# Conformer and forgetting-attention trunk: the shared filter sum moved to ScalarE and GpSimd ahead of the chunk, the memory matrices in split passes

## The chip, the core and the metric

The kernel runs on one core of a Trainium2 chip. Its time is the device time of one execution in microseconds. The engines are TensorE (PE; PEld for its weight loads), VectorE (DVE), ScalarE (ACT), GpSimd (POOL) and the DMA queue of SyncE (SP).

## What is computed

```python
for l in range(2):                                  # layer 0: convolution, layer 1: attention
    if l == 0:                                      # Conformer convolution
        u = h @ w_pw1 + b_pw1                       # 1024 tokens x 1024 -> 2 x 1024
        u = a * sigmoid(gate)
        u = causal depthwise convolution, 31 taps per channel, + b_dw
        x = x + silu(layernorm(u)) @ w_pw2 + b_pw2
    else:
        x = x + fox_attention(rmsnorm(x))           # 16 heads, shared keys and values
    mem_n = rmsnorm(mem)                            # 256 memory tokens
    k, v = mem_n @ w_k, mem_n @ w_v                 # 4 heads of 256
    x = x + softmax(q @ k.T) @ v @ w_o              # cross-attention, q = rmsnorm(x) @ w_q
    x = x + relu(rmsnorm(x) @ w1)**2 @ w2           # 4096 wide
return rmsnorm(x)
```

All is float32. A product may be taken in one pass over plain float32 operands, or each operand is split into a high part (type fp32r) and a low part (the rest), and three passes low x high, high x low, high x high are summed.

## The kernel before

Channels lie on the 128 partitions, tokens on the free axis; the 1024 channels make 8 chunks and the 1024 tokens two halves of 512. This text is about the first stage, `conv_layer`, in the first 527 us of the span; what follows it (memory attention, feed-forward, attention) is not touched.

For each chunk `gated_unit` makes the gated input u: four products of 24 matmuls (128x512, split operands), a sigmoid on ACT and a combining step on DVE for each half of the tokens. The tokens are stored as even and odd ones. `convolve` then filters the chunk: with d0 and d1, two differences of even and odd tokens, and `both`, a shared sum of 16 terms, every output half is `both` plus 16 (first half) or 15 (second half) terms from d0 or d1. Each term is one DVE instruction (`scalar_tensor_tensor`: source times a tap plus the running sum). After the last chunk `layer_norm` works on each half, and the product with `pw2` follows.

Beside it runs `memory_matrices`, a generator: for each of 2 layers and 4 heads it makes kt and vt (memory tokens times w_k, w_v), and from them with w_q and w_o the matrices mqk and mvo, which are stored to DRAM through a tile `o` with 2 buffers. It is advanced by one step (kt; vt; the w_q part; the w_o part) with each `next(prep)`: twice for each chunk, and what is left after `layer_norm`. The weights come through tiles `praw`.

The kernel is written in a tile language: instructions of one engine stay in the order that a scheduler fixes when the kernel is built, engines wait for one another by semaphores, and a tile's buffer is taken again when its last reader is done. Many short-lived tiles share one group of 4 buffers (`tag="t"`), taken in turn in the order of the program. PSUM has 8 banks; the preparation had 4 of them, the gate 2, small things 2.

Of the kernel before, what the change touches and what calls it, by code (L numbers as in the profile page):

```python
# [86 lines left out]
def trunk(ctx, tc, a, out):  # L87
# [98 lines left out]
    def add_squares(acc, ch):  # L186

        sq = nrm.tile([P, HALF], F32, name="sq", tag="t", bufs=4)
# [103 lines left out]

    def conv_layer(pm, prep):
        with tc.tile_pool(name="conv", bufs=2) as cp:
# [90 lines left out]

    def convolve(cp, m, u, sums):


        n, k = S // 2, TAPS // 2
        even, odd = u[:, 0, :], u[:, 1, :]  # L390
        d0 = cp.tile([P, n + k], F32, name="d0")
        d1 = cp.tile([P, n + k - 1], F32, name="d1")
        dve.tensor_tensor(d0, even[:, : n + k], odd[:, : n + k], op=ALU.subtract)
        dve.tensor_tensor(d1, even[:, 1 : n + k], odd[:, : n + k - 1], op=ALU.subtract)
        both = cp.tile([P, n], F32, name="both")
        dve.tensor_scalar(
            both, odd[:, :n], sums[:, 0:1], col("dw_b", m), op0=ALU.mult, op1=ALU.add
        )
        for j in range(1, k + 1):
            dve.scalar_tensor_tensor(  # L400
                both, odd[:, j : j + n], sums[:, j : j + 1], both, op0=ALU.mult, op1=ALU.add
            )
        out = [X[:, m, sl] for sl in HALVES]
        for s, d, taps in ((0, d0, k + 1), (1, d1, k)):
            y = both
            for j in range(taps):
                w = col("dw_w", m * TAPS + 2 * j + s)
                dve.scalar_tensor_tensor(  # L408
                    out[s], d[:, j : j + n], w, y, op0=ALU.mult, op1=ALU.add
                )  # L410
                y = out[s]

# [20 lines left out]
    def memory_matrices(pp, pq, layer):  # L433
# [3 lines left out]

        def get(src):
            raw = pp.tile([P, NCH, P], F32, name="praw", bufs=3)
            nc.sync.dma_start(raw, src)  # L440
            return raw

        mem = pp.tile([P, NCH, MEM], F32, name="mem", bufs=1)
        nc.sync.dma_start(mem, a["memT"])
        if layer == 0:
            r = inverse_rms([mem[:, c, :] for c in range(NCH)], RMS_EPS)
# [3 lines left out]
        for c in range(NCH):  # L450
            act.activation(mem[:, c, :], mem[:, c, :], AF.Copy, scale=col(f"src{layer}", c))
        for h in range(MEM_HEADS):
            kv = []
            for w, n in ((wk, "kt"), (wv, "vt")):
                t = bank(pq).rearrange("p (c m) -> p c m", c=2)
                for c in range(2):
                    x = get(w[2 * h + c])
                    product(t[:, c, :], [((x[:, k, :],), (mem[:, k, :],)) for k in range(NCH)])
                o = pp.tile([P, 2, MEM], F32, name=n, bufs=1)
                if w is wk:  # L460
# [8 lines left out]
                kv.append(o)  # L469
                yield  # L470
            kt, vt = kv
            for j in range(2):

                x = get(wq[h, j])
                for g in range(2):
                    t = bank(pq).rearrange("p (f m) -> p f m", f=2)
                    o = pp.tile([P, 4, P], F32, name="o").rearrange("p (f b) n -> p f (b n)", f=2)
                    for f in range(2):
                        product(t[:, f, :], [
                            ((x[:, 4 * c + 2 * g + f, :],), (kt[:, c, :],)) for c in range(2)  # L480
                        ])
# [6 lines left out]
            for j in range(2):  # L488

                x = get(wo[h, j])  # L490
                for mc in range(2):
                    t = bank(pq)
                    product(t, [
                        (
                            (vt[:, c, mc * P : (mc + 1) * P],),
                            (x[:, 4 * c : 4 * c + 4, :].rearrange("p b n -> p (b n)"),),
                        )
# [864 lines left out]

    with prep_pools(4) as pools, banks(2) as pm:
        conv_layer(pm, chain(*(memory_matrices(*pools, l) for l in range(2))))
    sums = mem_attention(0)
# [80 lines left out]
```

## Time and profile before

| | |
|---|---|
| median of 3 runs | 2822.05 us (2818.59 to 2823.66) |
| the profiled execution | 2825.31 us, span 2823.3 us |
| busy in the span | PE 2740.8 us, PEld 2261.3, DVE 2030.9, ACT 1278.3, POOL 703.1 |
| 80 to 388 us (filters of the 8 chunks) | PE 303.89 of 308, DVE 302.63, ACT 63.08, POOL 0.75 |
| 388 to 431 us (layer norm) | PE 41.68 of 43, DVE 31.63, ACT 27.98, POOL 2.01 |
| 431 to 527 us (pw2) | PE 96.00 of 96, DVE 41.30, ACT 33.10, POOL 0 |

Rows of groups give the line, engine, operation, output and inputs, the count after x, then the busy time in us, the mean duration of one in ns, and the idle time before them with what ended it. Matmuls are pipelined, so the mean of one is longer than the distance from one to the next. A plain float32 matmul shows as two records. Rows of a timeline give start in us, length in us, and the instructions that were merged. In rows of the order that the scheduler fixed, a name's number tells tiles of the same name apart.

### The profile page before, as it was taken

The numbers are of one execution on the slowest core, as the hardware profiler recorded it, in microseconds if no ns is written. First come the engines' busy times: TensorE is split into PE (matmuls) and PEld (weight loads), VectorE is DVE, ScalarE is ACT, GpSimd is POOL, SyncE is SP. The second block draws the span as 40 slices with busy tenths as digits, with TensorE's granted clock in tenths as the row PEclk, the third lists the DMA queues.
The fourth block names the chain that finished last, engine by engine and source line by source line (L and its number), as shares of the span: only waits on it lengthen the run. The fifth ranks groups of instructions, "written<-read, shape, count | busy, mean of one in ns | idle before, by whom it ended". The sixth has DMA issues, their size and how long they took to land.

```text
span 2823.3 us, 36214 instructions
## 1 busy us (share of the span) xinstructions
PE 2740.8 (97%) x12968; PEld 2261.3 (80%) x12968; DVE 2030.9 (72%) x3358; ACT 1278.3 (45%) x2293; POOL 703.1 (25%) x473
## 2 busy tenths in 40 slices
PE   8999999999999999999899999989999999989998
PEld 6777777888888877888688888878888788878886
DVE  5999984555776576777788888875546855577776
ACT  5212143433555553333466666673423655543332
POOL 0000000000065625774000000000000365525773
PEclk9999999999999999999899999999999999999999
DMA  6334364322165585652222221243213455655651
GB/s 219 120 119 135 114 206 124 101 90 70 65 230 177 178 309 187 227 199 89 69 68 70 57 65 55 69 136 98 94 64 105 149 176 190 218 208 197 227 201 61
DMA packets 165428, 390.68 MB, mean 138 GB/s; under 512 B 17264, under 2 KB 46192, under 8 KB 164992
## 3 DMA queue, kind: packets, MB, share of 16 engines
q1 hardware_dynamic: 165248, 388.37, 40.9%
q8 instruction: 102, 1.67, 0.2%
q14 instruction: 78, 0.64, 0.1%
HBM read 270.79 MB, written 113.31 MB: 136 GB/s over the span
## 4 chain that ended last, share of the span: by engine, by line
PE 74%; DVE 12%; ACT 5%; DMA 5%; issue 3%; POOL 1%; SPq 0%; DVEq 0%; POOLq 0%; ACTq 0%
PE mm L1070 34%; PE mm L269 29%; PE mm L1255 5%; DVE w L148 2%; DVE op L148 2%; DVE x L408 1%; PE mm L1341 1%; DVE x L1310 1%; DMA ua<-x 1%; ACT x L1315 1%; PE mm L1353 1%; PE mm L1354 1%; DVE both L400 1%; DVE wl L148 1%; ACT pth L151 1%
## 5 line engine op out<-in xcount | busy, mean ns | idle before, releaser
L1070 PE MATMUL mm<-op,w 128*128 128x512 f32 x5424 | 1242.4, 391 | 24.5 <-ACT m L955 8.7
L1070 PEld LDWEIGHTS mm<-op,w 128*128 128x128 f32 x5424 | 1020.5, 189 | 243.2 <-ACT m L955 9.6
L269 PE MATMUL mm<-op,wh 128*128 128x512 f32 x1056 | 330.5, 394 | 4.2 <-DVE op L148 4.2
L148 DVE TENSOR_TENSOR w<-r,w 128x512 fp32r<-128x512 f32 x264 | 262.6, 998 | 30.5 <-ACT w L653 30.5
L653 ACT CAST w<-r 128x512 fp32r<-128x512 f32 x264 | 163.3, 622 | 262.0 <-PE mm L1070 233.2
L269 PEld LDWEIGHTS mm<-op,wh 128*128 128x128 f32 x1056 | 200.2, 190 | 48.5 <-DVE op L148 6.5
L1255 PE MATMUL mm<-op,wh 128*128 128x512 f32 x736 | 231.4, 396 | 0.0
L148 DVE TENSOR_TENSOR w<-t,w 128x512 fp32r<-128x512 f32 x180 | 178.2, 1005 | 63.2 <-ACT w L653 63.1
L269 PE MATMUL mm<-op,wl 128*128 128x512 f32 x528 | 210.5, 400 | 7.1 <-DVE wl L148 6.2
L207 POOL TENSOR_TENSOR r<-v,mhalf 128x4 f32<-128x4 f32 (+1 forms) x15 | 16.8, 1117 | 741.0 <-DVE v L205 741.0
L647 POOL TENSOR_TENSOR t<-r,t 128x512 f32<-128x512 f32 x104 | 174.9, 1681 | 91.4 <-DVE w L148 54.2
L653 ACT CAST w<-t 128x512 fp32r<-128x512 f32 x180 | 112.0, 622 | 169.8 <-PE mm L1070 140.6
L151 ACT CAST wh<-raw 128x1024 fp32r<-128x1024 f32 x96 | 100.7, 1050 | 193.8 <-PE mm L269 97.5
L865 POOL TENSOR_TENSOR x<-x,x 128x512 f32<-128x512 f32 x112 | 160.2, 1455 | 112.6 <-ACT x L878 101.6
L967 DVE TENSOR_TENSOR x<-mm,x 128x512 f32<-128x512 f32 x160 | 109.5, 684 | 91.1 <-PE mm L1070 73.7
L1255 PEld LDWEIGHTS mm<-op,wh 128*128 128x128 f32 x736 | 139.2, 189 | 26.7
L269 PE MATMUL mm<-op,xsh 128*128 128x512 f32 x512 | 158.0, 393 | 0.0
L1255 PE MATMUL mm<-op,wl 128*128 128x512 f32 x368 | 155.0, 421 | 1.9 <-ACT q L1275 1.9
L151 ACT CAST pth<-mm 128x512 fp32r<-128x512 f32 (+1 forms) x224 | 105.9, 495 | 108.5 <-PE mm L556 80.8
L408 DVE SCALAR_TENSOR_TENSOR x<-d,par,x 128x512 f32<-128x512 f32 x232 | 154.5, 746 | 0.0
L647 POOL TENSOR_TENSOR t<-r,r 128x512 f32<-128x512 f32 x52 | 80.2, 1542 | 295.1 <-DMA r<-in_ff_w 191.0
L1315 ACT ACTIVATE x<-x,nb 128x128 f32<-128x128 f32 (+7 forms) x128 | 99.5, 778 | 109.3 <-DVE nb L1313 100.0
(188 smaller groups left out, 4689.6 us busy)
## 6 DMA issues: line engine op xcount, KB each, us to landing
r<-in_ff_w SPq DMA_DIRECT2D x128, 512.0 KB, 4.0
op<-ua SPq DMA_DIRECT2D x80, 512.0 KB, 6.8
us<-x SPq DMA_DIRECT2D x128, 256.0 KB, 2.9
op<-us SPq DMA_DIRECT2D x64, 512.0 KB, 5.6
raw<-mvo SPq DMA_DIRECT2D x32, 512.0 KB, 3.4
ua<-ul SPq DMA_DIRECT2D x64, 256.0 KB, 2.2
ua<-uh SPq DMA_DIRECT2D x60, 256.0 KB, 2.3
raw<-in_pw SPq DMA_DIRECT2D x24, 512.0 KB, 4.7
```

The costliest lines, as they stand in the source:

```text
L148: dve.tensor_tensor(lo, src, hi.bitcast(F32), op=ALU.subtract)
L151: act.copy(hi, src)
L269: pe.matmul(out_ps, x, y, start=i == 0, stop=i == len(terms) - 1)
L400: dve.scalar_tensor_tensor(both, odd[:, j : j + n], sums[:, j : j + 1], both, op0=ALU.mult, op1=ALU.add)
L408: dve.scalar_tensor_tensor(out[s], d[:, j : j + n], w, y, op0=ALU.mult, op1=ALU.add)
L647: (dve if g in (2, 3, UP, UP + 1) else pool).tensor_tensor(t, raws[g, x], raws[g, y], op=ALU.subtract)
L653: act.copy(highs[n][0], raws[steps[n][:2]])
L865: eng.tensor_tensor(u[g, x], y1, y2, op=op_)
L967: dve.tensor_tensor(v, sums[key], v, op=ALU.add)
L1070: pe.matmul(sums[key], y, z, start=first and i == 0, stop=n == last_of[key] and i == len(terms) - 1, skip_group_check=True,)
L1255: pe.matmul(t, x, y, start=n == 0, stop=n == len(terms) - 1)
L1315: act.activation(x[:, :n], x[:, :n], AF.Exp, bias=nb, accum_out=rs)
```

## The change

- The shared sum becomes a function of its own, `shared_sum`: ACT multiplies (16 instructions), and POOL adds (15), in place of 16 instructions on DVE. It is issued, with the gate of the next chunk, before the filters of the chunk at hand. The products of ACT go through the tiles of the group "t".
- The two filter chains of a chunk run one after the other with their running sum in one PSUM bank (pool `pc`), no longer in X; only the last step writes X. d0 and d1 have one buffer instead of two.
- The preparation takes its products in three split passes. Weights come as two half pieces, each cast on ACT (high part), the low part subtracted on DVE for the first half piece and on POOL for the second. kt and vt are split too (kt by way of a tile of the group "t"), and the memory tokens. Its PSUM banks go from 4 to 3.

```diff
@@ conv_layer
+            ready = u, shared_sum(cp, 0, u, pairs[:, 0])
             for m in range(NCH):
-                if m:
-                    u = padded()
-                    for sl in HALVES:
-                        gated_unit(pm, cp, m, ahead, hs, u[:, :, PAD // 2 :], sl)
+                now = ready
                 if m + 1 < NCH:
                     ahead = gate_weights(m + 1)
                 for _ in range(2):
                     next(prep, None)
-                convolve(cp, m, u, pairs[:, m])
+                if m + 1 < NCH:
+                    u = padded()
+                    for sl in HALVES:
+                        gated_unit(pm, cp, m + 1, ahead, hs, u[:, :, PAD // 2 :], sl)
+                    ready = u, shared_sum(cp, m + 1, u, pairs[:, m + 1])
+                convolve(cp, pc, m, *now)
...
+    def shared_sum(cp, m, u, sums):
+        n, k = S // 2, TAPS // 2
+        odd = u[:, 1, :]
+        both = cp.tile([P, n], F32, name="both")
+        act.activation(both, odd[:, :n], AF.Identity, scale=sums[:, 0:1], bias=col("dw_b", m))
+        for j in range(1, k + 1):
+            t = nrm.tile([P, HALF], F32, name="tap", tag="t", bufs=4)
+            act.activation(t, odd[:, j : j + n], AF.Copy, scale=sums[:, j : j + 1])
+            pool.tensor_tensor(both, both, t, op=ALU.add)
+        return both
@@ convolve
-        out = [X[:, m, sl] for sl in HALVES]
+        acc = bank(pc)
         for s, d, taps in ((0, d0, k + 1), (1, d1, k)):
             y = both
             for j in range(taps):
+                o = X[:, m, HALVES[s]] if j == taps - 1 else acc
                 w = col("dw_w", m * TAPS + 2 * j + s)
-                dve.scalar_tensor_tensor(
-                    out[s], d[:, j : j + n], w, y, op0=ALU.mult, op1=ALU.add
-                )
-                y = out[s]
+                dve.scalar_tensor_tensor(o, d[:, j : j + n], w, y, op0=ALU.mult, op1=ALU.add)
+                y = acc
@@ memory_matrices
         def get(src):
-            raw = pp.tile([P, NCH, P], F32, name="praw", bufs=3)
-            nc.sync.dma_start(raw, src)
-            return raw
+            halves = []
+            for i in range(2):
+                raw = half(src[:, 4 * i : 4 * i + 4, :])
+                hi, lo = (pp.tile([P, NCH // 2, P], F32R, name=f"p{x}", bufs=3) for x in "hl")
+                act.copy(hi, raw)
+                (pool if i else dve).tensor_tensor(lo, raw, hi.bitcast(F32), op=ALU.subtract)
+                halves.append((hi, lo))
+            return halves
...
+                hi, lo = (pp.tile([P, 2, MEM], F32R, name=n + y, bufs=1) for y in "hl")
                 if w is wk:
...
+                        o = nrm.tile([P, HALF], F32, name="kt", tag="t", bufs=4)
+                        o = o.rearrange("p (c m) -> p c m", c=2)
                         dve.tensor_tensor(o, t, rb, op=ALU.mult)
+                        split(hi, lo, o)
                 else:
-                    act.copy(o, t)
+                    split(hi, lo, t)
...
-    with prep_pools(4) as pools, banks(2) as pm:
+    with prep_pools(3) as pools, banks(2) as pm, banks(1) as pc:
```

Three places show how the order on the engines moves. First DVE, from the end of one chunk's filters to the next chunk's. Before, the u of a chunk, d0, d1, the shared sum (L396, L400) and the filters (L408) follow one another:

```order
L354 TENSOR_TENSOR acc1_565<-acc1_565,x31_84 128x512
L370 SCALAR_TENSOR_TENSOR u_1382<-mm_1411,par_63,sg_1384 128x2x256
L370 SCALAR_TENSOR_TENSOR u_1382<-mm_1464,par_63,sg_1437 128x2x256
L148 TENSOR_TENSOR wl_1493<-raw_1490,wh_1492 128x1024
L148 TENSOR_TENSOR wl_1499<-raw_1496,wh_1498 128x1024
L393 TENSOR_TENSOR d0_1548<-u_1382 128x527
L394 TENSOR_TENSOR d1_1549<-u_1382 128x526
L396 TENSOR_SCALAR both_1552<-u_1382,sums_227,par_63 128x512
L400 SCALAR_TENSOR_TENSOR both_1552<-u_1382,sums_227,both_1552 128x512 x14
L370 SCALAR_TENSOR_TENSOR u_1602<-mm_1631,par_63,sg_1604 128x2x256
L400 SCALAR_TENSOR_TENSOR both_1552<-u_1382,sums_227,both_1552 128x512
L408 SCALAR_TENSOR_TENSOR x40_85<-d0_1548,par_63,both_1552 128x512
```

Now u_1720 is the fourth chunk's u, whose second half is written here in the midst of the third chunk's second chain (filters are L418, their sum mm_1879), and both_1828 is the sum that ACT and POOL make from it:

```order
L374 SCALAR_TENSOR_TENSOR u_1720<-mm_1802,par_63,sg_1775 128x2x256
L418 SCALAR_TENSOR_TENSOR mm_1879<-d1_1876,par_63,mm_1879 128x512
L148 TENSOR_TENSOR wl_1922<-raw_1919,wh_1921 128x1024
L418 SCALAR_TENSOR_TENSOR mm_1879<-d1_1876,par_63,mm_1879 128x512
L410 TENSOR_TENSOR d0_2236<-u_1720 128x527
L418 SCALAR_TENSOR_TENSOR mm_1879<-d1_1876,par_63,mm_1879 128x512 x10
L418 SCALAR_TENSOR_TENSOR x21_82<-d1_1876,par_63,mm_1879 128x512
L358 TENSOR_TENSOR acc1_782<-acc1_782,x21_82 128x512
L411 TENSOR_TENSOR d1_2237<-u_1720 128x526
L458 TENSOR_TENSOR pl_2020<-praw_2017,ph_2019 128x512
L418 SCALAR_TENSOR_TENSOR mm_2240<-d0_2236,par_63,both_1828 128x512
```

The first filter of the fourth chunk now stands 18 instructions behind the u from which its sum is made, and waits for POOL. From the third chunk's first filter to this u_1720 the order has 18 filters, 2 lows of half pieces (L458), the low of vt, an acc, a wl and two u.

Second, POOL over the first chunks. Before it has the powers of the norms and the clearing of u's edge:

```order
L207 TENSOR_TENSOR r<-v,mhalf 128x2
L207 TENSOR_TENSOR r<-v,mhalf 128x4 x2
L301 MEMSET u 128x2x15 x6
L207 TENSOR_TENSOR r<-v,mhalf 128x4 x4
L207 TENSOR_TENSOR rf<-v,mhalf 128x4
```

Now the 15 adds of a chunk's sum (L402) and the lows of the second half pieces (L458) take turns:

```order
L458 TENSOR_TENSOR pl<-praw,ph 128x512 x3
L402 TENSOR_TENSOR both<-both,tap 128x512 x15
L301 MEMSET u 128x2x15
L458 TENSOR_TENSOR pl<-praw,ph 128x512 x4
L402 TENSOR_TENSOR both<-both,tap 128x512 x15
L301 MEMSET u 128x2x15
L458 TENSOR_TENSOR pl<-praw,ph 128x512 x5
L402 TENSOR_TENSOR both<-both,tap 128x512 x15
```

Some lows stand behind a sum's 15 adds. PE needs the first of them before it can go on to the next chunk's gate.

Third, the layer norm, on PE and ACT. Before, PE's matmuls of the norm (L158, L167) lie among products of the preparation (mm_2712, mm_2718, mm_2741, and mm_2766 and mm_2775 for w_q), which wait for none of it:

```order
L158 MATMUL mm_2355<-mean_col_70,acc_2332 128x1 x4
L269 MATMUL mm_2712<-praw_2704,vt_2648 128x512
L167 MATMUL mm_2364<-ident_65,r_2362 128x128 x4
L158 MATMUL mm_2402<-mean_col_70,acc1_565 128x1 x4
L269 MATMUL mm_2718<-mem_1964,praw_2719 128x256 x3
L167 MATMUL mm_2408<-ident_65,nm_2401 128x128 x4
L269 MATMUL mm_2718<-mem_1964,praw_2719 128x256 x5
L269 MATMUL mm_2718<-mem_1964,praw_2729 128x256 x8
L269 MATMUL mm_2741<-mem_1964,praw_2742 128x256 x8
```

Now six groups of the norm follow one another, and the first product behind them takes kth_3836, the high part of a kt (pw2 starts 23 rows further on):

```order
L158 MATMUL mm_3586<-mean_col_70,acc0_781 128x1 x4
L167 MATMUL mm_3592<-ident_65,nm_3585 128x128 x4
L158 MATMUL mm_3628<-mean_col_70,acc_3605 128x1 x4
L167 MATMUL mm_3637<-ident_65,r_3635 128x128 x4
L158 MATMUL mm_3675<-mean_col_70,acc1_782 128x1 x4
L167 MATMUL mm_3681<-ident_65,nm_3674 128x128 x4
L269 MATMUL mm_3931<-kth_3836,pl_3922 128x256
```

On ACT that kth_3836 stands behind the squares of the second half's norm (L182), because kt and those squares take buffers of the group "t" in turn, and an o is followed by the whole second half's silu (L318) and casts:

```order
L182 ACTIVATE t_3708<-x51_88 128x512
L182 ACTIVATE t_3711<-x61_90 128x512
L182 ACTIVATE t_3714<-x71_92 128x512
L151 CAST kth_3836<-kt_3838 128x512
L516 ACTIVATE o_3932<-mm_3931,par_63 128x256
L318 ACTIVATE x01_78<-x01_78,par_63 128x512
L318 ACTIVATE x11_80<-x11_80,par_63 128x512
```

At this point of PE's order 10 of the 32 preparation steps are still to come (w_q and w_o of the second layer's second head, all of its third and fourth), and all of pw2; before, it was the 4 steps of the fourth head and all of pw2.

More of the change, by code (lines that the diff above doesn't have):

```diff
@@ L436, in memory_matrices, with half @@
         ad, vd = mats[layer]
+        def half(src):
+            raw = pp.tile([P, NCH // 2, P], F32, name="praw", bufs=4)
+            nc.sync.dma_start(raw.rearrange("p k n -> p (k n)"), src.rearrange("p k n -> p (k n)"))
+            return raw
         def get(src):
[L439 to L444 removed]
+            halves = []
[6 more added lines that the diff above has]
+            return halves
+        memh, meml = (pp.tile([P, NCH, MEM], F32R, name=f"mem{x}", bufs=1) for x in "hl")
+        sums = None
+        for c in range(NCH):
+            if c % 2 == 0:
+                two = half(a["memT"][:, c : c + 2, :]).rearrange("p (c k) n -> p c (k n)", c=2)
+            ch, g = two[:, c % 2, :], col(f"src{layer}", c)
+            if layer == 0:
+                sums = add_squares(sums, ch)
+            act.activation(memh[:, c, :], ch, AF.Copy, scale=g)
+            dve.scalar_tensor_tensor(
+                meml[:, c, :], ch, g, memh[:, c, :].bitcast(F32), op0=ALU.mult, op1=ALU.subtract
+            )
         if layer == 0:
[L446 removed]
+            with tc.high_priority(offset=SMALL_FIRST):
+                r = rms_of_sums(sums, RMS_EPS)
             rt = const.tile([P, MEM // P], F32, name="mem_r")
```

35 lines of the change are left out of this document (13 added, 22 removed).

## Prediction

> **What bounds the kernel now.** I read the stretches of the first stage first, then its groups, then DVE's and PE's timelines there. In a stretch's row: length, busy us (count) of PE, PEld, DVE, ACT, POOL, granted clock, DMA share, GB/s.
>
> ```profile
> 80.00:388.00 308.00, 303.89 (x1285) 240.85 (x1284) 302.63 (x436) 63.08 (x105) 0.75 (x6) 1.00 0.43 137
> 388.00:431.00 43.00, 41.68 (x201) 32.01 (x199) 31.63 (x54) 27.98 (x51) 2.01 (x2) 1.00 0.61 187
> 431.00:527.00 96.00, 96.00 (x414) 76.95 (x412) 41.30 (x55) 33.10 (x50) 0.00 (x0) 1.00 0.33 101
> ```
>
> While the chunks are filtered PE and DVE are both full and POOL is idle. The layer norm's waits are filled on PE by preparation, and pw2 then runs without a break. So two things set the stage's end at 527 us: DVE's filters, and the sum of PE's work.
>
> ```profile
> 275.99 8.63 DVE L400 SCALAR_TENSOR_TENSOR both<-u,sums,both 128x512 f32<-128x512 f32 x11
> 289.66 12.67 DVE L408 SCALAR_TENSOR_TENSOR x<-d,par,x 128x512 f32<-128x512 f32 x19
> 315.42 8.63 DVE L400 SCALAR_TENSOR_TENSOR both<-u,sums,both 128x512 f32<-128x512 f32 x11
> 366.54 1.42 DVE L408 SCALAR_TENSOR_TENSOR x<-d,par,both 128x512 f32<-128x512 f32 x2
> 526.98 1.02 PE L158 MATMUL mm<-mean_col,acc 128*128 128x1 f32 x8
> ```
>
> One chunk takes 315.42 - 275.99 = 39.4 us. The adds of the shared sum, each waiting for the one before, come every 0.78 us; the filters, two chains in alternation, every 0.67. The last chunk's filters begin at 366.54; from there it is 160.4 us to the next stage's first norm on PE, just behind pw2.
>
> **The change, part by part.**
>
> *Split passes, on PE.*
>
> ```profile
> 344.43 13.98 PE L269 MATMUL mm<-mem,praw 128*128 128x256 f32 x64
> 338.42 6.17 PE L269 MATMUL mm<-praw,vt 128*128 128x512 f32 x14
> 574.92 5.75 PE mm L269 x48
> L269 PE MATMUL mm<-mem,praw 128*128 128x256 f32 x512 | 116.7, 386 | 9.1 <-ACT mem L451 8.7 <-DMA praw<-in_mem_wk 0.5
> L269 PE MATMUL mm<-kt,praw 128*128 128x256 f32 x256 | 61.2, 385 | 6.0 <-ACT o L483 4.5 <-DMA praw<-in_mem_wq 1.4
> L269 PE MATMUL mm<-praw,vt 128*128 128x512 f32 x128 | 59.1, 594 | 0.0
> ```
>
> A plain product of 256 columns is two records of 0.218 us; the split passes of 48 matmuls at 256 columns in the third row (memory attention) take 0.12 each. At 512 columns it is two of 0.44 against three of 0.23 (96.0 us / 414 in pw2's stretch). Before: 768 x 0.218 + 128 x 0.44 = 224 us. After: 1152 x 0.12 + 192 x 0.23 = 182. PE has 42 us less to do. That is the whole possible gain, if PE is never kept waiting longer than now.
>
> *The shared sum, off DVE.* DVE loses 8 x (15 x 0.78 + 0.5) = 98 us. It gains 64 lows, 16 lows of kt and vt, 16 of memory tokens (about 55 us at 0.61), and since the filters are now one dependent chain in one bank, 8 x 31 x (0.78 - 0.67) = 27 us. So DVE is freed of little. The weight is on what the sum now costs in time:
>
> ```profile
> L647 POOL TENSOR_TENSOR t<-r,t x104: 1286/1622/2302, 790.9 to 2768.8; 128x512 f32<-128x512 f32 x104
> L647 POOL TENSOR_TENSOR t<-r,r x52: 1286/1301/2285, 789.4 to 2754.4; 128x512 f32<-128x512 f32 x52
> 902.21 1.30 POOL L647 TENSOR_TENSOR t<-r,r 128x512 f32<-128x512 f32 x1 [9.72 <-DMA r<-in_ff_w]
> 903.58 1.62 POOL L647 TENSOR_TENSOR t<-r,t 128x512 f32<-128x512 f32 x1
> 12.69 1.65 ACT L182 ACTIVATE t<-x 128x512 f32<-128x512 f32 x3
> ```
>
> A two-input POOL instruction of this size takes 1.29 us at least (min/median/max in ns), and the one depending on it starts 1.37 after it did. From the second half of u to a ready sum: two ACT instructions at about 0.6, then 15 x 1.37 = 20.6; together 22 us, where DVE needed 12. ACT's later products wait for POOL (4 buffers), so casts, sigmoids and evacuations queue behind them; they have the rest of the chunk.
>
> POOL and DVE also disturb each other:
>
> ```profile
> L148 DVE TENSOR_TENSOR w<-r,w 128x512 fp32r<-128x512 f32 x264 | 262.6, 998 | 30.5 <-ACT w L653 30.5
> L148 DVE TENSOR_TENSOR op<-h,op 128x512 fp32r<-128x512 f32 x16 | 10.9, 689 | 0.5 <-ACT op L222 0.4
> L967 DVE TENSOR_TENSOR x<-mm,x 128x512 f32<-128x512 f32 x160 | 109.5, 684 | 91.1 <-PE mm L1070 73.7
> ```
>
> With two inputs in SBUF the same subtraction takes 998 ns where POOL works beside it and 689 where it doesn't; with one input in PSUM it stays at 684. POOL's median is 0.34 above its minimum. Five DVE instructions of the former kind (wl, d0, acc, d1, a low) lie within a sum: 0 to 5 x 0.34 = 1.7 us; I take 0.9. The filters read their sum from PSUM and should be left alone.
>
> The Trainium skill (SBUF — State Buffer, "Who interferes with whom") says that a DVE instruction with two SBUF inputs and a reading GpSimd instruction block each other fully, and that one with a single SBUF input does not contend. The rows agree on who is hit, but show a third of an instruction instead of a whole one. By the rule the five would cost a sum about 3.6 us, and the result below would be some 19 us later.
>
> *The loop that this closes.* DVE runs in order, and a chunk's first filter waits for its sum. Behind it come (order above) 18 filters, 4 short subtractions or adds, a wl and two u until the next chunk's u is complete, from which the next sum starts:
>
> ```profile
> 311.35 2.34 DVE L148 TENSOR_TENSOR wl<-raw,wh 128x1024 fp32r<-128x1024 f32 x2
> 391.55 4.88 DVE L314 TENSOR_TENSOR x<-x,mm 128x512 f32<-128x512 f32 x8 [1.27 <-PE mm L167]
> 22.04 0.16 DVE L205 TENSOR_SCALAR v<-mm 128x4 f32<-128x4 f32 x1 [0.52 <-PE mm L158]
> ```
>
> 18 x 0.78 + 4 x 0.61 + 1.17 + 2 x 0.67 = 19.0 us. So a chunk needs at least 22.9 + 19.0 = 42 us, against 39.4. A filter that writes PSUM is not in the trace. Bounds: 0.67 (the filters now), and 0.78 + 0.16 (a whole tiny instruction on top); reading PSUM costs nothing visible (684 against 689), so I take 0.78. Ends: -2 and +3 us a chunk.
>
> PE's path round the same loop is as long. In every other chunk the kt and vt parts stand ahead of the gate, with a low that POOL makes only after the 15 adds: 1.4 (low) + 60 x 0.12 + 60 x 0.23 + u = 23.1 us. I count 4 chunks of 46 and 3 of 42: 310 us for the seven steps, where it was 275. PE would idle some 8 us in each, and then:
>
> ```profile
> 34.00:42.00 8.00, 6.24 (x27) 5.03 (x27) 7.05 (x11) 5.99 (x13) 0.00 (x0) 1.00 0.82 260
> 42.00:50.00 8.00, 7.37 (x27) 6.15 (x28) 0.89 (x3) 2.06 (x5) 1.01 (x1) 0.59 0.46 138
> ```
>
> After waits of 2 us around 42 the granted clock falls to 0.59 for 8 us, 3.3 us of work. Left out of the sum; it is upward reach, 0 to 4 x 3.3.
>
> The Trainium skill (TensorE: Matmul & The Clock Gate, Part 1) says that an idle window of about 3.4 us halves the clock until a like window of work. The trace agrees on the halving, and the rule speaks against this change, which makes such gaps; by it each costs about 1.7 us, some 7 us in all.
>
> *Start and end.*
>
> ```profile
> 75.94 0.75 DVE L370 SCALAR_TENSOR_TENSOR u<-mm,par,sg 128x512 f32<-128x512 f32 x1 [2.56 <-PE mm L269]
> 396.34 5.46 DVE L183 TENSOR_TENSOR acc<-acc,t 128x512 f32<-128x512 f32 x7
> 405.59 0.69 DVE L317 TENSOR_TENSOR x<-x,mm 128x512 f32<-128x512 f32 x1 [2.34 <-PE mm L167]
> 430.72 3.08 DVE L317 TENSOR_TENSOR x<-x,mm 128x512 f32<-128x512 f32 x5 [2.33 <-PE mm L167]
> 441.25 1.30 DVE L148 TENSOR_TENSOR op<-x,op 128x512 fp32r<-128x512 f32 x2 [1.20 <-ACT op L151]
> 386.57 1.89 PE L269 MATMUL mm<-kt,praw 128*128 128x256 f32 x8
> 399.53 2.74 PE L269 MATMUL mm<-praw,vt 128*128 128x512 f32 x6
> 30.14 0.33 SPq L440 DMA_DIRECT2D praw<-in_mem_wo x1
> ```
>
> The first u is complete at 76.7; I leave that (more casts, less PE). The first sum is ready at 76.7 + 22 = 99, the last at 99 + 310 = 409 = B, where filters began at 366.5 before.
>
> Then the norm is interleaved with the last filters. Up to the first kt behind it DVE has 31 filters (16 x 0.78, 15 in alternation x 0.67), 9 lows and accs and 8 L314 at 0.61, 7 L183 at 0.78 (38.5 us), the wait for the power (401.8 to 405.6, 3.8), 24 more at 0.61 and 5 at 0.78 (18.6), and kt: B + 61.5; cast, B + 62. PE has nothing before that: its norm matmuls, and then a product that needs this kt. It idles about 40 us, where it was 1.3 in the norm's stretch. Next ACT takes the second half's silu and casts (430.7 to 442.5, 11.8 us, starting about B + 67), and with 3 PSUM banks for the preparation PE gets through some 10 us of work until B + 79. Left are 10 preparation steps (57 us) and pw2 (384 x 0.23 = 88), less 10: B + 214. If the o stores pace a w_q and w_o pair as before (386.6 to 402.3, 15.7 us for 11.4 of work), B + 225. I take B + 218 = 627 us.
>
> Covered: 64 more weight loads at 0.33 us on SP (behind them wait o stores and gate weights; 21 us over 400); 128 casts on ACT at 0.55, 70 us beside ACT's 63 in 308. If ACT's cover goes, the sigmoids come late and with them u.
>
> **The sum.** 627 - 527 = +100 us on the profiled 2825.3, that is 2925; the median of the runs is 3.3 lower: 2922.
>
> **Rivals.**
> - *The norm is still covered.* If PE's leftover is small because preparation ran ahead during the slower chunks, the end is B + 161 = 570: +43, 2865. For it: PE has 8 us a chunk to spare. Against: its order is fixed, 10 steps stand behind the norm.
> - *PE's work alone decides: faster.* PE is at 303.9 of 308, and 42 us of its work go: 2822 - 42 = 2780. It needs every new wait to hide. The point is 39.4 us a chunk with the norm covered: then nothing is lost, and the POOL adds would have to come every (39.4 - 19 - 1.2) / 15 = 1.28 us on DVE's path, and 1.0 on PE's. The shortest seen is 1.29 alone, 1.37 in a chain.
> - *It is worse.* PSUM filters at 0.94 (+3 a chunk, +5 at the end), full contention (+0.8) and the slow clock (+3.3 in four) make +45: 2967.
>
> **How the numbers follow.** A change under 0.2% (6 us) can't be told from none here. Forecast 0.75 (2885 to 2960, from -2 us a chunk, the start and end 20 us shorter, to +3 a chunk and +15 at the end); norm covered 0.10; worse 0.10; faster 0.03; within 0.2%, where small gains and losses cancel, 0.02. The range takes in the covered norm and the worse case's near side: 2862 to 2968.
>
> **What would show it.** Right: DVE waiting for POOL's `both` 8 us or more in each chunk; chunks 42 to 46 us apart; L402 at 1.37 or more; a PE gap of 40 us after the last filters, ended by the cast of kt; more PE time at a clock of half. Wrong: L402 near 0.9, u complete much earlier than 19 us behind the first filter, or preparation matmuls between the norm's.

## The result, and the profile after

The changed kernel takes 2988.27 us (2986.05 to 2991.57, 4 runs), the kernel before 2822.86 on the same chip: ratio 1.059, 95% interval 1.0571 to 1.0608. The forecast was 2922, its range ended at 2968: the sign was right, and the loss was 165 us instead of 100, beyond the range.

The stretches of the changed kernel, cut at the first filter of the first and of the last chunk and where pw2 runs and ends (columns as in the prediction: length, busy us of PE, PEld, DVE, ACT, POOL, granted clock, DMA share, GB/s):

```profile
105.03:452.10 347.07, 255.44 (x1268) 216.48 (x1269) 256.71 (x321) 164.52 (x262) 186.16 (x142) 0.86 0.29 91
452.00:520.00 68.00, 26.92 (x161) 25.36 (x160) 57.67 (x92) 29.78 (x47) 7.49 (x6) 0.62 0.21 64
520.00:600.00 80.00, 72.32 (x446) 62.17 (x446) 31.83 (x43) 48.06 (x87) 23.34 (x18) 0.96 0.61 188
600.00:692.00 92.00, 89.58 (x396) 73.09 (x396) 36.36 (x48) 29.12 (x43) 4.74 (x3) 1.00 0.34 103
692.00:2986.00 2294.00, 2228.86 (x10775) 1856.57 (x10774) 1604.44 (x2733) 1110.26 (x2011) 692.08 (x453) 0.99 0.40 137
```

The same cuts of the kernel before:

```profile
91.97:366.54 274.57, 270.91 (x1145) 214.34 (x1144) 269.70 (x388) 57.84 (x96) 0.75 (x6) 1.00 0.40 128
527.00:2823.00 2296.00, 2232.58 (x10808) 1859.61 (x10807) 1611.85 (x2743) 1115.44 (x2021) 696.80 (x454) 0.99 0.40 137
```

What follows the first stage is unchanged (2294 us against 2296), so the whole loss lies in it. The seven steps from first filter to first filter take 347 us (49.6 each) instead of 275 (39.2). Before, PE and DVE were both full there; now neither is: PE is busy 74% of the time at a clock of 0.86, DVE 74%. Both wait. Behind the last chunk's first filter come 238 us instead of 160, with PE at 26.92 of 68 us in the norm. Against the forecast the first filter is 6 us late (105 for 99), the steps 37 us long (347 for 310), the rest 20 us (238 for 218).

The waits from 80 to 480 us (waiting engine and line, releaser; us in total, times, longest):

```profile
POOL pl L458 <- ACT ph L457: 69.5, 20, 11.3
ACT tap L401 <- POOL both L402: 55.1, 80, 1.2
DVE pl L458 <- ACT ph L457: 48.2, 14, 7.8
PE mm L269 <- POOL pl L458: 46.8, 10, 13.0
PE mm L269 <- ACT o L516: 40.2, 4, 17.0
DVE mm L418 <- POOL both L402: 29.4, 2, 18.8
```

The forecast expected the last row in every chunk, 8 us or more. It is there in two of eight. In the others DVE is still at a low, a kt or the filters before when the sum gets ready, and PE waits for POOL's lows and ACT's evacuations (copies of its results out of PSUM). In six of PE's ten waits for a POOL low, 44.3 of the 46.8 us, POOL made that low directly behind the 15 adds of a sum. DVE's timeline just ahead of chunk 2's filters shows DVE's part:

```profile
198.49 0.69 DVE L498 TENSOR_TENSOR kt<-mm,mem_rs 128x512 f32<-128x512 f32 x1 [7.86 <-POOL both L402]
199.10 1.27 DVE L411 TENSOR_TENSOR d<-u 128x526 f32<-128x526 f32 x1
200.29 1.75 DVE L458 TENSOR_TENSOR pl<-praw,ph 128x512 fp32r<-128x512 f32 x1
201.96 1.76 DVE L148 TENSOR_TENSOR ktl<-kt,kth 128x512 fp32r<-128x512 f32 x1
203.64 1.76 DVE L458 TENSOR_TENSOR pl<-praw,ph 128x512 fp32r<-128x512 f32 x1
205.32 0.75 DVE L418 SCALAR_TENSOR_TENSOR mm<-d,par,both 128x512 f32<-128x512 f32 x1
```

kt waits for a POOL add, since its tile is one of the four that the tap products use. And beside POOL's adds a DVE subtraction with two SBUF inputs takes 1.75 us, not 0.69.

### The profile page after: what moved, and what is told of

Its sections match the earlier page's. It is cut to its first block, busy times and chain, and to the rows that moved or that the text cites. A ratio compares the mean times of both kernels' runs of the same rounds, so it can differ in the third digit from the quotient of the medians.

```text
span 2986.3 us, 37930 instructions
## 1 busy us (share of the span) xinstructions
PE 2743.1 (92%) x13416; PEld 2293.7 (77%) x13416; DVE 2044.2 (68%) x3326; ACT 1444.4 (48%) x2557; POOL 950.4 (32%) x657
## 4 chain that ended last, share of the span: by engine, by line
PE 62%; DVE 8%; ACT 5%; DMA 3%; issue 3%; POOL 0%; SPq 0%; DVEq 0%; POOLq 0%; ACTq 0%
PE mm L1103 34%; PE mm L269 17%; PE mm L1288 5%; DVE op L148 2%; DVE w L148 1%; PE mm L1374 1%; DVE x L1343 1%; PE mm L1386 1%; PE mm L1387 1%; ACT x L1348 1%; PE mm L1338 1%; ACT pth L151 1%; PE mm L1339 1%; ACT wh L151 1%; DMA r<-in_ff_w 1%
## 5 line engine op out<-in xcount | busy, mean ns | idle before, releaser
L269 PEld LDWEIGHTS mm<-op,wh 128*128 128x128 f32 x1056 | 202.4, 192 | 49.6 <-DVE op L148 8.4
L402 POOL TENSOR_TENSOR both<-both,tap 128x512 f32<-128x512 f32 x120 | 162.0, 1350 | 95.6 <-ACT tap L401 86.9
L418 DVE SCALAR_TENSOR_TENSOR mm<-d,par,mm 128x512 f32<-128x512 f32 x216 | 162.7, 753 | 4.6
```

What stands on the lines that cost most here:

```text
L269: pe.matmul(out_ps, x, y, start=i == 0, stop=i == len(terms) - 1)
L402: pool.tensor_tensor(both, both, t, op=ALU.add)
L418: dve.scalar_tensor_tensor(o, d[:, j : j + n], w, y, op0=ALU.mult, op1=ALU.add)
```

## The experiments

All compare with the kernel before on the same chip. "Step" is the mean distance of the chunks' first filters, "last" the start of the last chunk's first filter, "behind" what comes from there to the end of the stage (span less 2296 us); the three come from each run's DVE timeline.

| run | us | ratio (interval) | step | last | behind |
|---|---|---|---|---|---|
| before | 2822.86 | | 39.2 | 367 | 161 |
| changed kernel | 2988.27 | 1.059 (1.0571 to 1.0608) | 49.6 | 452 | 238 |
| split preparation alone | 2985.96 | 1.0577 (1.0551 to 1.0602) | 50.2 | 457 | 231 |
| sum alone | 2931.37 | 1.0385 (1.0361 to 1.0409) | 47.1 | 424 | 210 |
| sum alone, u ahead | 2892.11 | 1.0253 (1.0222 to 1.0284) | 39.6 | 388 | 207 |
| the same, taps in X | 2878.68 | 1.0206 (1.0183 to 1.0228) | 38.2 | 376 | 201 |
| split alone, lows as ACT casts | 2900.67 | 1.029 (1.0268 to 1.0311) | 40.5 | 379 | 222 |
| the same, preparation first | 2872.96 | 1.0175 (1.0151 to 1.0198) | 41.2 | 386 | 192 |
| changed, lows on DVE | 2961.71 | 1.0497 (1.0467 to 1.0526) | 47.5 | 439 | 224 |
| changed, kt in its own buffer | 2962.37 | 1.0494 (1.0473 to 1.0515) | 48.5 | 438 | 228 |
| changed, preparation first | 2962.28 | 1.0507 (1.0485 to 1.053) | 49.4 | 452 | 213 |

**The two halves by themselves.** The sum alone keeps `shared_sum`, the order and the PSUM filters, with `memory_matrices` as before; the split alone is the kernel before with the new `memory_matrices` (and its four PSUM banks).

```diff
# split alone: conv_layer and convolve of before, and
-        d1 = cp.tile([P, n + k - 1], F32, name="d1")
+        d1 = cp.tile([P, n + k - 1], F32, name="d1", bufs=1)
```

> The split preparation alone; the shared sum stays on DVE, behind the chunk's differences, as before (d1 has one buffer). Theory A (the 22 us of the sum on ACT and POOL lie in series with the 19 us from a chunk's first filter to the next u, and close a loop): without that loop the loss goes; DVE, which was full, gets 4 lows and a kt or vt low more in a chunk, some 3 us, and PE has 42 us less: 2800 to 2850 us. Rival S (the split preparation itself holds PE, by its casts, its lows and their queues): more than half of the loss stays, above 2900 us.

> The shared sum on ACT and POOL and the gate ahead, with the plain preparation of before (no casts, no lows, kt in its own tile). Theory A by my sum of 22.9 + 19.0 alone: steps of 42 us, first filters at about 99, and the norm covered since kt stands ahead of the norm's end on DVE: 2840 to 2860 us. Rival B (what the sum costs beyond those 42 us comes from casts, lows and evacuations of the split preparation that queue behind taps on ACT and adds on POOL): the same 2840 to 2860, since those are gone here. Rival C (POOL's adds slow DVE's instructions by contention, and that makes the steps of 50): steps stay near 48, above 2890 us.

Each half loses most of it: +167 us the split (2985.96 - 2818.95), +112 the sum, +165 both. So theory A fell as the whole reason: without any sum on POOL the loss is as large. The two losses do not add up either. The stretches of the split alone and of the sum alone, first filter to first filter:

```profile
105.06:456.78 351.72, 262.53 (x1301) 221.94 (x1299) 308.07 (x433) 92.31 (x156) 83.66 (x38) 0.87 0.29 95
```

```profile
94.29:423.95 329.66, 251.11 (x993) 197.12 (x992) 218.24 (x274) 125.66 (x193) 142.17 (x111) 0.88 0.25 84
```

In the split alone DVE has 38 us more to do than before (308.07 against 269.70) and 39 us more idle (43.65 against 4.87). Its groups there, and two of PE's waits in that stretch:

```profile
L400 DVE SCALAR_TENSOR_TENSOR both<-u,sums,both 128x512 f32<-128x512 f32 x105 | 88.1, 839 | 2.6
L450 DVE TENSOR_TENSOR pl<-praw,ph 128x512 fp32r<-128x512 f32 x31 | 25.6, 835 | 26.8 <-ACT ph L449 26.7
```

```profile
PE mm L269 <- POOL pl L450: 46.0, 13, 8.9
PE mm L269 <- DVE wl L148: 30.4, 3, 11.7
```

A low of a half piece costs 0.8 us of DVE's time, and as much again of waiting for its cast, with the filters standing behind it. The gate's lows (wl) stand in the same queue, and PE waits 30.4 us for three of them. An add of the shared sum takes 0.84 us, where it took 0.75 before. The casts in turn wait for PE, 72.4 us in 29 waits, since a piece's high part has three buffers and PE is the last to read them; no run gave the pieces more buffers, so that remains a rival for a part of this loss. POOL's lows are late for another reason. One line's durations (ns, min/median/max), and the timelines of DVE and POOL around one of them:

```profile
L450 POOL TENSOR_TENSOR pl<-praw,ph x64: 1260/1294/8570, 13.8 to 600.2; 128x512 fp32r<-128x512 f32 x64
```

```profile
159.20 9.36 DVE L408 SCALAR_TENSOR_TENSOR x<-d,par,x 128x512 f32<-128x512 f32 x14
```

```profile
163.83 7.09 POOL L450 TENSOR_TENSOR pl<-praw,ph 128x512 fp32r<-128x512 f32 x2 [11.65 <-ACT ph L449]
```

```profile
169.73 0.39 PE L269 MATMUL mm<-memh,pl 128*128 128x256 f32 x1 [3.81 <-POOL pl L450]
```

Two lows that take 2.6 us elsewhere take 7.09: the first 5.84, beside DVE's unbroken filters (two SBUF inputs, end 168.56), the second 1.28 behind them. PE waits for the first.

The sum alone shows the loop by itself. DVE's wait for the sum over the seven steps, its timeline of a chunk, and PE's row in it:

```profile
DVE mm L418 <- POOL both L402: 120.7, 8, 17.4
```

```profile
188.22 0.76 DVE L418 SCALAR_TENSOR_TENSOR mm<-d,par,both 128x512 f32<-128x512 f32 x1 [14.20 <-POOL both L402]
189.02 11.05 DVE L418 SCALAR_TENSOR_TENSOR mm<-d,par,mm 128x512 f32<-128x512 f32 x14
...
201.56 0.74 DVE L374 SCALAR_TENSOR_TENSOR u<-mm,par,sg 128x512 f32<-128x512 f32 x1
...
211.46 0.74 DVE L374 SCALAR_TENSOR_TENSOR u<-mm,par,sg 128x512 f32<-128x512 f32 x1
```

```profile
202.36 0.79 PE L269 MATMUL mm<-op,wl 128*128 128x512 f32 x1 [8.69 <-DVE u L374]
```

The first u stands behind 17 filters. Until it has run, PE lacks one of the gate's two banks and idles 8.69 us; then it makes the last of the four products (24 matmuls, to 209.7), and the second u follows at 212.2: 24.0 us behind the filter, where the forecast had 19.0. With 22.9 us from there to the next filter that is the step of 47. Rival C had named such a time and such steps, but for another reason: DVE's instructions slowed by POOL. The filters on this path take 0.79 us each, and the instructions that are slowed (d 1.67 and 1.07 us on average, acc 1.07) are not what it waits for.

**Opening the queues.** Lows on DVE: `dve.tensor_tensor(lo, raw, ...)` for both half pieces. Taps in X: the chunks of X that no filter has written yet take the tap products (12 of 15 in chunk 2, 4 in chunk 6; the 13 and 5 of the expectation are a slip), the rest the four buffers.

```diff
-            t = nrm.tile([P, HALF], F32, name="tap", tag="t", bufs=4)
+            i = j - 1 + 2 * m
+            if i < 2 * NCH:
+                t = X[:, NCH - 1 - (j - 1) // 2, HALVES[j % 2]]
+            else:
+                t = nrm.tile([P, HALF], F32, name="tap", tag="t", bufs=4)
```

> The changed kernel with all lows of the weight pieces on DVE, none on POOL. Rival B: PE waited 46.8 us in 10 waits for POOL's lows, which stand behind the 15 adds; they go, DVE has 4 lows (2.4 us) more in a chunk: 2945 to 2970 us. Theory A alone: the loop is sum plus filters, lows do not matter: 2980 to 2995 us.

> The changed kernel with the tap products in idle chunks of X (all 15 have a place of their own up to chunk 0, 13 in chunk 2, 5 in chunk 6, then the four buffers), so that ACT is done with them after about 10 us instead of 18 and isn't held by POOL. Rival B: the evacuations (PE waited 40.2 us for o) and casts that stood behind the taps come 8 us earlier in the first five chunks: 2940 to 2965 us. Theory A alone: POOL's 15 adds set the sum as before: 2978 to 2990 us.

> Both queues opened at once: all lows on DVE and the tap products in idle chunks of X. Theory D (PE is held by the preparation's lows behind POOL's adds and by its evacuations and casts behind ACT's taps; opening one queue alone leaves the other): beyond the -27 us of the lows alone another 15 to 40, 2920 to 2945 us. Theory A (the sum's 22 us in series with the filters sets the step, whatever queues behind it): 2955 to 2965 us, as with the lows alone.

> Plain preparation, sum on ACT and POOL with the gate ahead, tap products in idle X. In the run without X PE waited 46 us in 5 waits for o (longest 18.8) and steps were 47.1 us. Theory D: in the first chunks those waits shrink by the 8 us that ACT is free earlier: 2890 to 2915 us. Theory A: the step is the sum of 22.5 us and 24.3 us from filter to u, 2925 to 2935 us as without.

The lows gave their 27 us: 2961.71. The taps gave nothing, three times: 2987.87 in the changed kernel, 2961.85 with the lows on DVE, 2934.14 in the sum alone (against 2931.37), although ACT was done with them after 10 us instead of 18 (chunk 2 of the changed kernel). So ACT held by the taps is not what set the steps in these kernels, and theory D fell in that part. For POOL's queue the 27 us stand, though that run takes POOL's slowed lows away with the queue; 14 of them come off the seven steps (333 us instead of 347).

**The order behind the last chunk, and kt's buffer.**

```diff
+            for _ in prep:
+                pass
             ss = operands()
             for s in range(2):
                 layer_norm(s, acc[s])
-            for _ in prep:
-                pass
# and, another run
-                        o = nrm.tile([P, HALF], F32, name="kt", tag="t", bufs=4)
+                        o = pp.tile([P, HALF], F32, name="kt", bufs=1)
```

> The changed kernel with the remaining preparation written ahead of the layer norm, so that DVE makes three kt between the last filters and the norm's first sums; the chunks are untouched. If the hole of PE in the norm (10 us of work in the 40 from 480, clock 0.50) comes from kt's place on DVE, it goes and the end comes 25 to 45 us earlier: 2943 to 2963 us. Rival: the norm itself comes later by the lows and kts now ahead of it, and pw2 with it: above 2975 us.

> The changed kernel with kt's tile in a buffer of its own and not among the four that the tap products use (DVE waited 7.9 us for POOL's adds at kt once, and 10.7 for PE). If the shared buffers hold kt: 2965 to 2982 us. If not, and the tail stays, since kt stands behind the norm on DVE in any case: 2983 to 2993 us.

Both give 26 us (for kt's buffer slightly more than expected). Preparation first fills the hole, in which PE worked 9.91 us at a clock of 0.50 before: in the 40 us from 480 PE works

```profile
480.00:520.00 40.00, 36.06 (x250) 32.38 (x251) 23.05 (x33) 22.77 (x41) 14.75 (x11) 1.00 0.75 231
```

and the steps stay. With kt in its own buffer the first filter comes at 98.4, the 99 of the forecast, since the norm's squares at the start, which shared the four buffers with kt, no longer come behind it (L183 begins at 15.0 instead of 24.6 us, kt is at 22.4 instead of 21.8); the step falls by 1.1 us and the rest by 10.

**u ahead of the filters.** The two u of the next chunk are held ahead of the chunk's filters on DVE, so that the next sum runs beside them.

```diff
+                with in_order((dve.engine,)):
                     if m + 1 < NCH:
                         u = padded()
...
                     convolve(cp, pc, m, *now)
```

> Plain preparation, sum on ACT and POOL; DVE's order held as the code is written, so that both u of the next chunk stand ahead of a chunk's filters (in the run without it the first u stood behind 15 filters and the second 10 us later, behind PE's last gate product). Theory E (the ring is sum 22.5, 15 filters ahead of the first u, PE's product for the second half, then the next sum: 47 us): the next sum now runs beside the filters, nothing closes within a chunk, PE's work of 39.4 us decides: steps of 39 to 42, 2830 to 2860 us. Rival D (PE is held by evacuations behind ACT's taps): steps of 45 or more, above 2885 us.

> The changed kernel with both u of the next chunk ahead of a chunk's filters on DVE; preparation and the norm as they are. Theory E: steps fall from 49.6 to 42 to 44 us, the tail stays: 2935 to 2960 us. Rival S (the split preparation holds DVE and PE by itself, as in the run of the split alone with its steps of 50 us): 2975 us or more.

> The same with the remaining preparation written ahead of the norm, which alone gave 26 us. If steps and tail are two separate losses, both gains add: 2910 to 2935 us. If they share a cause, the gain is that of the larger one: 2935 to 2960 us.

> The same and all lows on DVE, tap products in idle X. Theory E with DVE as the next bound (some 38 to 40 us of work in a chunk): 2880 to 2915 us. Rival S: above 2930 us.

> The sum alone with u ahead of the filters, and tap products in idle X, so that ACT is not held. Theory D on top of E (with the ring open, PE's 44 us of waits for o behind the taps are what is left): 2850 to 2872 us. Rival (POOL's or DVE's part is next, so that ACT's freedom buys nothing, as in the run without u ahead): 2882 to 2895 us.

In the sum alone this takes 39 us away; the step falls from 47.1 to 39.6 as theory E has it, but the time missed its 2830 to 2860: 2892.11, where rival D had it, though not with rival D's steps of 45. PE still waits for evacuations behind the taps (without, then with the taps in X):

```profile
PE mm L269 <- ACT o L492: 44.3, 9, 17.1
```

```profile
PE mm L269 <- ACT o L496: 36.3, 7, 17.1
```

With the taps in X 8 us of these waits go, and the median falls by 13 us (2878.68, short of the 2850 to 2872 expected). The intervals of the two ratios touch, so that ACT's queue counts once the loop is open is likely, not shown. The steps are then shorter than before the change, and the stretches say where the rest is:

```profile
109.19:376.45 267.26, 230.85 (x948) 180.34 (x947) 220.56 (x272) 119.14 (x193) 146.20 (x111) 0.94 0.33 107
376.45:577.00 200.55, 188.69 (x796) 147.91 (x794) 96.28 (x142) 72.61 (x118) 2.02 (x2) 0.97 0.44 142
```

PE does 231 us of work beside the filters instead of 271, and the missing 40 come behind them (201 instead of 161). So what the shorter steps win is lost again behind them, where PE has to do the work that it didn't do beside the filters.

In the changed kernel the same order is worse, 3009.07 (1.0675, 1.0651 to 1.07). Its first filter has to wait for the next chunk's u, and that stands behind lows and kt on DVE:

```profile
103.56 1.36 DVE L459 TENSOR_TENSOR pl<-praw,ph 128x512 fp32r<-128x512 f32 x1 [17.06 <-ACT ph L458]
111.67 0.69 DVE L499 TENSOR_TENSOR kt<-mm,mem_rs 128x512 f32<-128x512 f32 x1 [6.75 <-PE mm L269]
...
131.28 0.75 DVE L375 SCALAR_TENSOR_TENSOR u<-mm,par,sg 128x512 f32<-128x512 f32 x1 [2.55 <-PE mm L269]
```

The first filter is at 133 instead of 105 and the step is still 49.2. With preparation first it is 2975.84 (1.0564, 1.054 to 1.0587), above both of its expectations, and with all lows on DVE and the taps in X as well 2939.14 (1.0431, 1.0406 to 1.0457), where rival S had it. So the loop of sum and filters sets the step of the sum alone. In the changed kernel opening it leaves the step as long as the split alone has it (50.2), which speaks for the split preparation (rival S).

**Gates two chunks ahead**, with three u buffers, lows on DVE, taps in X and preparation first:

> Gates two chunks ahead (three u buffers, pieces in three buffers), so that a sum has a whole chunk's filters to finish beside; lows on DVE, taps in idle X, remaining preparation ahead of the norm. Theory A and D alike: no chain of sum, filter and u closes within a chunk any more; DVE then sets the step with 24.2 us of filters, 2.4 of wl, 1.5 of u, 1.2 of d, 1.3 of acc, 6 of lows and kt, about 37 us; steps of 38 to 42 us: 2820 to 2860 us. Rival C (DVE's two-input instructions are slowed by POOL's adds to 1.75 us, some 12 of them in a chunk): steps of 48, 2890 us or more.

2918.32 (1.0345, 1.033 to 1.0361), steps of 44.9: the best of the kernels with both halves, and still 99 us behind the kernel before. The time is rival C's and not the 2820 to 2860 of the theories; the steps lie between the two. In its steps DVE is the bound, 299.58 of 314.21 us busy, and its lows are the second largest group, at 1.02 us each where 0.69 is the time of one alone:

```profile
L468 DVE TENSOR_TENSOR pl<-praw,ph 128x512 fp32r<-128x512 f32 x75 | 76.1, 1023 | 7.8 <-ACT ph L467 7.6
```

**The lows taken away.** In the split alone a second cast by ACT stands in the place of each weight piece's low. The kernel then leaves the low parts of the weights out and holds the high part twice; PE's products are as many as before.

```diff
-                (pool if i else dve).tensor_tensor(lo, raw, hi.bitcast(F32), op=ALU.subtract)
+                act.copy(lo, raw)
```

> The split preparation alone (sum on DVE as before), with a second cast by ACT in the place of each low of a weight piece, so that neither DVE nor POOL makes them; the low parts then hold other numbers. Theory S1 (the lows are what holds the chunks at 50 us: 3.7 us of DVE's work and 3.8 of its waits for their casts in each, and PE's 45 us of waits for POOL's, which come late): steps fall to 41 to 44 us, the hole in the norm stays: 2920 to 2950 us. Rival S2 (casts on ACT, half pieces and kt's place hold PE, not the lows): 2965 us or more.

> The split alone with second casts by ACT in the place of the lows (the low parts hold other numbers), and the remaining preparation written ahead of the norm. If the hole of PE behind the chunks (some 75 us idle between 353 and 440) is a matter of order: 2820 to 2855 us, near before although PE's 42 us are saved. Rival (as in the second layer's run, the preparation's steps from piece to piece then delay the norm itself): 2885 us or more.

85 us go: 2900.67, 19 below the range of S1. The steps are 40.5. In the first six of them (first row) PE is full again, at full clock; then it has little to do:

```profile
95.35:340.11 244.76, 235.34 (x1271) 201.37 (x1270) 237.56 (x346) 117.21 (x213) 0.76 (x6) 1.00 0.41 132
340.00:440.00 100.00, 20.77 (x99) 18.54 (x97) 88.18 (x137) 26.34 (x41) 1.01 (x1) 0.56 0.05 16
```

PE has run ahead of DVE; next in its order stand the norm's sums, which wait for the last filters (waits from 80 to 440 us):

```profile
PE mm L158 <- DVE acc L354: 51.3, 1, 51.3
```

With preparation first as well, 28 us come back: 2872.96, between the 2820 to 2855 of a pure matter of order and the 2885 of the rival. What holds the rest stays open: of its 49 us 5 lie ahead of the first filter, 14 in the steps (41.2 instead of 39.2) and 31 behind them.

**Splitting only where DVE has room.** The kernel before with only the second layer's preparation split (its last 12 of 16 steps are written behind the chunks) and preparation first. Its high and low pieces have two buffers each, not three. The control changes the order alone.

> The kernel before with only the second layer's preparation in split passes (12 of its 16 steps run behind the chunks, where DVE is busy 31 of 43 and 41 of 96 us), and the remaining preparation written ahead of the norm. PE has 21 us less to do; if DVE has room there and the norm is covered: 2800 to 2815 us, faster than before by 0.2 to 0.8%. Rival (the norm comes later by lows and kts, or is not covered): 2825 to 2860 us.

> The control: the kernel before with only the order changed (remaining preparation written ahead of the norm). PE was full there anyway: 2818 to 2832 us. If the norm comes later and pw2 with it: 2835 us or more.

The control is the same as before, 1.0005 (0.9991 to 1.0019). The split of one layer costs 105 us, 2925.21 (1.0373, 1.0351 to 1.0395), against an expected gain, and more than the rival's 2860 at most. POOL's and DVE's timelines at the first split pieces:

```profile
293.19 15.45 POOL L453 TENSOR_TENSOR pl<-praw,ph 128x512 fp32r<-128x512 f32 x1 [7.30 <-ACT ph L452]
```

```profile
287.01 19.29 DVE L408 SCALAR_TENSOR_TENSOR x<-d,par,x 128x512 f32<-128x512 f32 x29
```

One low takes 15.45 us on POOL; it ends 2.3 us behind DVE's run of 29 filters (306.30). And in the norm the steps of preparation, each with a cast and a low ahead of its matmuls, now hold up the norm: its sums (L183) start only

```profile
477.49 0.69 DVE L501 TENSOR_TENSOR kt<-mm,mem_rs 128x512 f32<-128x512 f32 x1 [1.02 <-PE mm L269]
...
480.58 1.48 DVE L183 TENSOR_TENSOR acc<-acc,t 128x512 f32<-128x512 f32 x2
```

behind that kt, 80 us after the last filter. None of the runs is faster than the kernel before.

## Why the prediction was wrong, point by point

- *Split passes, 42 us less for PE.* With the lows out of the way PE ran ahead of DVE at full clock, as that saving lets it; a pass of 256 columns takes 0.12 us there, as counted. None of it reached the end.
- *The lows, "55 us at 0.61", set against 98 us that DVE loses.* This is the step that failed; in the sum it is the 310 us of the seven steps, which came as 347. The lows were counted as work to be added up, with 1.4 us of POOL's on PE's path. Three things were missing: a low waits for its cast, and DVE's filters wait behind it (48 us from 80 to 480); POOL's lows wait for the adds, and PE for them (46.8 us); and they are slowed by the other engine. Taken away in the split alone they give back 85 of its 167 us, with no sum on POOL at all. In the changed kernel, moving POOL's lows to DVE gave 27 us, 14 of them in the steps. The part of the two engines was not run separately in the split alone, nor were the lows taken off both in the changed kernel, so how much of the changed kernel's 37 us in the steps is theirs stays open, as do the 80 us that the split alone still loses without them.
- *The sum takes 22 us.* Right: 22.4 us from the complete u to the filter in chunk 0; the 15 adds take 20.8 us there and 21.0 to 22.0 in the other chunks.
- *Contention 0.9 us a chunk.* Mis-sized. The 0.34 was POOL's excess in another stage; the pair here costs DVE 1.75 - 0.69 = 1.06 us. From 105 to 452 us DVE's two-input instructions took some 28 us more than with POOL idle: 12 acc by 0.49, 14 d by 0.43, 30 lows by 0.31, 14 first filters by 0.33, and 2 for wl and ktl, from the group means of the two kernels; 4 us a step. How much of it lay on the path is not shown. The rule of the Trainium skill cited (SBUF — State Buffer, "Who interferes with whom"), a full block, was nearer than the row that I preferred.
- *The loop, 22.9 + 19.0 = 42.* The loop exists, as the sum alone shows, but its second part is 24.0: I counted DVE's instructions up to the second u and left out PE's last product between the two u. In the sum alone this second mistake by itself makes the steps 47.1 where 42 was forecast. Opening the loop is worth 39 us there. In the changed kernel that leaves the steps as they are (49.2), and a later first filter makes it 21 us slower.
- *Four steps of 46 and three of 42.* They came 42 to 58, mean 49.6. The three long ones (52.5, 53.7, 58.0) are those where a kt stands just ahead of the first filter; the four others are 42.1 to 47.9. So long and short do alternate, as forecast for the chunks with kt and vt, but the long ones are 6 to 12 us longer than 46.
- *The clock left out, 0 to 4 x 3.3.* The granted clock was 0.86 in the steps and 0.62 in the norm, against 1.00 where PE hardly waited (600 to 692 us). The sum should have carried it.
- *First filter at 99.* 105; with kt's tile out of the shared buffers 98.4. That kt shares them was in the diff, and I left the start as it was.
- *The end, B + 218 with a hole of 40 us ended by kt's cast.* The mechanism was right: kt comes 64 us behind the last chunk's first filter (61.5 forecast), PE's hole is ended by its cast (row below), and with preparation written ahead of the norm 26 us come back. What follows kt takes 174 us instead of 156. PE waits for lows nine times there up to 600 us, 6.5 us in all; the rest of the difference was not traced.

```profile
517.57 1.01 PE L269 MATMUL mm<-kth,pl 128*128 128x256 f32 x3 [16.87 <-ACT kth L151]
```

- *Rivals.* "The norm is still covered" and "PE's work alone decides" did not come; "worse" did, 21 us beyond its 2967, but not for its first reason: the PSUM filters took 0.79 us each, close to the 0.78 assumed. Contention and the slow clock, its two others, were there.

## What to carry to other kernels

Where two engines are both full and feed each other in order, work moved to idle engines has to be priced by what queues in front of it and who stands behind the result, not by its busy time: both halves of this change relieved an engine and each alone lost 4 to 6%. Test the halves of such a change apart; a cheaper product that needs a cast and a subtraction ahead of it was no gain here, where the subtraction stood in the queue of the engine that paces the loop. And shorter steps of the second engine gain little if PE idles in them, since its work then comes behind.

## What the runs showed of the hardware that was not expected

- POOL can be kept out for much longer than one DVE instruction. A subtraction of 1.26 us with two SBUF inputs took up to 8.57 us (split alone), and 15.45 in the run with one layer split, while DVE ran filters with two SBUF inputs without a gap; DVE's filters kept their distance of 0.66 us. With the filters' running sum in PSUM (the changed kernel) the longest such subtraction was 1.76 us. But there the filters are also one chain, each waiting for the one before. Beside the shared sum's adds in the split alone, such a chain with two SBUF inputs, POOL's subtractions took 1.3 to 1.8 us too, so it may be the gaps of a chain that let POOL in, and not PSUM; no run separates the two. The page of the Trainium skill cited above (SBUF — State Buffer, in its "Summary: rules for kernel authors") has the second to issue blocked until the first finishes; here POOL was held for many DVE instructions.
- The other way round, DVE's single two-input instructions beside POOL's chain of adds took up to 1.81 us instead of 0.69 to 0.75 (the changed kernel), and POOL's adds stayed at a median of 1.28.
